# One kernel, its first stage written out by hand: a hybrid encoder layer on one core

## The chip, the cores and the metric

The kernel runs on one core of a Trainium2 chip. A core has TensorE (matrix multiplication, accumulating in PSUM banks of 128 x 512 float32), VectorE, ScalarE and GpSimd, and queues that move data; here SyncE issues all of the transfers. Each engine runs its own list of instructions in order and waits on semaphores for the others. The metric is the device time of one execution in microseconds, lower is better.

## The reference

One layer over 2048 tokens of 1024 channels, all in float32. Only the head of it matters here:

```python
c_act = silu(c)                                   # 1024 values
shift, scale, gate = split(c_act @ ada_w + ada_b, 3)
h = layernorm(x) * (1 + scale) + shift            # 2048 x 1024
q_h, i_h, zf_fw, zf_bw, g_h, q_n, k_n, v_n, g_n = split(h @ w_in)   # 9216 columns
y = concat([hgrn2(q_h, i_h, zf_fw, zf_bw) * silu(g_h), natten(q_n, k_n, v_n, rpb) * silu(g_n)]) @ w_out
out = layernorm(ALPHA * x + gate * y) * ln_g + ln_b
```

`natten` is a two-dimensional neighbourhood attention with 16 heads of 64 channels (handled in 8 pairs), `hgrn2` a gated linear recurrence in both directions with 8 heads of 128. `rpb` is the attention's bias by relative position.

## The kernel before

**Tiling.** The 2048 tokens are two halves of 1024, and each half is two groups (g = 0, 1) of 512 rows. The 1024 channels are eight blocks k of 128. h is kept transposed, channels on partitions, as a sum of a rounded high part and a low part (`hts[g, k, 0]` and `[g, k, 1]`, both float32r, in rows `h`). Weights are split in the same way (`wh`, `wl`), and a product is three matmuls: high by high, low by high, high by low. `proj_mm` (L255) does that for one 128-column block of weights, one k and one group, 512 columns at a time; `vproj` (L268) does it for the attention's values, 256 columns at a time with h as the stationary operand.

**The first stage** (`startup`) makes h of the first half and, with the same steps, the attention's q, k and gate columns of head pair 0 for both groups. The rows of x come in tiles of 128 x 512 (`x_load`). `x_norm` takes their mean and variance on VectorE (L199, L200), makes the rates of four tiles together (L175 to L204) and scales all eight tiles of a group on ScalarE (L208). `h_piece` turns four tiles over with TensorE (L216, out of `ident`), applies shift and scale on ScalarE (L218), copies the high part (L220) and leaves the rest on VectorE (L223).

Shift and scale come from the modulation. `mod_init` makes silu(c), stores it to memory (`c_d`) and loads it back to all partitions (`cb`). `mods(k)` loads two 128 x 1024 blocks of `ada_w` (L144) and multiplies and sums each along its rows on VectorE (L145, rows `ada`). The loop over k does both groups at each k: the sums for k + 1, both groups' pieces for k + 1, then 18 matmuls of 512 columns for k.

**The second stage** (`first_half`) cuts the results into attention operands (`Prep`), runs `vproj` for the first two head pairs, and then goes through the eight pairs: `natten_woven` yields the attention's steps (scores L978 and L981, softmax L990 to L1000, turning L1022, the sums with the values V at L1041), and `weave` puts projections of the next pair between them, in proportion. `slots` holds the small jobs that lie beside: the gate's modulation, the lower bounds of the recurrence (`lower_bounds`), and h of the second half. The values go to memory (`nv`) and come back as `V`, and the bias tables are built in memory (`bias_fill`, `bias_tables`, `bias_pair`).

**What sets the order.** TensorE runs in the order in which the code calls it. The lists of VectorE, ScalarE and SyncE are put together by a scheduler, by its own estimate of when operands are ready; `pinned` operations keep their written order among themselves, and `high_priority` (the weights, `load_split` and `Chunks`) moves an operation up. That is why the first four loads of value weights stand at the head of SyncE's list before. `Chunks` is the feed of weights: four raw buffers (`WR`), split into high and low parts as the buffers of earlier ones come free.

## Time and profile before

| | us |
|---|---|
| median of three timed runs | 2703.81 |
| lowest and highest | 2697.77, 2707.67 |
| the profiled execution | 2706.45 |
| its span, first to last instruction | 2704.6 |
| TensorE busy in it | 2607.9 (96%) |
| VectorE, ScalarE busy | 1763.5 (65%), 1419.8 (52%) |

TensorE is busy for 96% of the span, with a mean granted clock of 0.99, so little is idle, and the place of it counts. The page's slices of 67.6 us show that the first holds most of what is missing. The other engines' shares say nothing by themselves: what they do in the first stage, where TensorE waits for them, is read from their timelines there. Line numbers in the rows below are those of the kernel before; the order of the changed kernel has its own.

### The profile page before, as it was taken

The page shows a single profiled execution, that of the slowest core. Times are in us where ns is not written, and L with a number is a line of the kernel's source. Part 1 is how long each engine was busy: PE and PEld are TensorE (multiplying, and loading weights), DVE is VectorE, ACT ScalarE, POOL GpSimd, SP SyncE. Part 2 cuts the span into 40 slices and gives each one's busy share as a digit, 9 for nine tenths or more (in the row PEclk, how much of TensorE's full clock was granted, in tenths as well). Part 3 has the DMA queues.
Part 4 walks back from the last instruction along what each step waited for, and adds up shares of the span by engine and source line. Part 5 has one row for each costly group of instructions (what it writes and reads, how often), then busy time and mean ns, then how long its engine had stood idle before and what let it go on. Part 6 is the DMA issues. An engine that isn't in the chain of part 4 may idle for free.

```text
span 2704.6 us, 46039 instructions
## 1 busy us (share of the span) xinstructions
PE 2607.9 (96%) x17328; PEld 2154.8 (80%) x17328; DVE 1763.5 (65%) x4351; ACT 1419.8 (52%) x2808; POOL 105.6 (4%) x142
## 2 busy tenths in 40 slices
PE   4999999989999999999999999999999999899998
PEld 3788888878888888888888888887777777678887
DVE  5435445467777778877777877555777778548443
ACT  4434444366666666666666666445666666431110
POOL 0000000000000000000000000000000000032221
PEclk9999999999999999999999999999999999899999
DMA  7565354312111126212221122354444445344331
GB/s 248 158 186 143 128 173 139 116 52 75 63 59 60 64 75 219 79 43 75 75 77 62 65 70 87 102 164 129 123 127 129 126 126 138 109 137 140 98 94 55
DMA packets 226846, 296.46 MB, mean 110 GB/s; under 512 B 28743, under 2 KB 117575, under 8 KB 226503
## 3 DMA queue, kind: packets, MB, share of 16 engines
q1 hardware_dynamic: 226623, 293.52, 35.0%
q8 instruction: 136, 2.23, 0.3%
q14 instruction: 87, 0.71, 0.1%
HBM read 218.24 MB, written 66.99 MB: 105 GB/s over the span
## 4 chain that ended last, share of the span: by engine, by line
PE 71%; DVE 2%; DMA 2%; ACT 1%; SPq 1%; issue 0%; DVEq 0%; ACTq 0%
PE pj L255 39%; PE ps L1333 4%; PE ps L1334 4%; PE ps L1335 4%; PE ps L1041 3%; PE ps L1022 3%; PE ps L455 2%; PE pj L268 2%; PE ps L447 1%; PE ps L978 1%; PE ps L981 1%; PE ps L522 1%; PE ps L546 1%; PE ps L494 1%; PE ps L548 1%; PE ps L620 1%
## 5 line engine op out<-in xcount | busy, mean ns | idle before, releaser
L255 PE MATMUL pj<-h,wh 128*128 128x512 f32 x4016 | 1287.3, 402 | 6.0 <-ACT wh L781 2.1
L255 PEld LDWEIGHTS pj<-h,wh 128*128 128x128 f32 x4016 | 727.4, 189 | 166.6 <-issue 21.5
L255 PE MATMUL pj<-h,wl 128*128 128x512 f32 x2008 | 788.5, 393 | 0.0
L255 PEld LDWEIGHTS pj<-h,wl 128*128 128x128 f32 x2008 | 377.9, 188 | 83.1 <-DVE wl L756 0.4
L995 ACT ACTIVATE pbuf<-pbuf,mx 128x480 f32<-128x480 f32 (+2 forms) x256 | 164.3, 643 | 180.1 <-DVE mx L990 179.4
L990 DVE CUSTOM_DVE_ANT_1 pbuf<-ps,bias 128x480 f32<-128x480 f32 (+2 forms) x256 | 144.0, 595 | 134.4 <-PE ps L981 119.6
L268 PE MATMUL pj<-wh,h 128*128 128x256 f32 x1024 | 197.4, 290 | 4.4 <-ACT vt L274 4.2
L268 PEld LDWEIGHTS pj<-wh,h 128*128 128x128 f32 x1024 | 165.0, 195 | 8.6 <-ACT vt L274 5.1
L245 ACT ACTIVATE wh<-wr 128x512 fp32r<-128x512 f32 x192 | 120.1, 626 | 79.7 <-PE pj L255 69.5
L246 DVE TENSOR_TENSOR wl<-wr,wh 128x512 fp32r<-128x512 f32 x192 | 131.6, 685 | 42.8 <-ACT wh L245 41.8
L268 PE MATMUL pj<-wl,h 128*128 128x256 f32 x512 | 146.5, 286 | 0.0
L1022 PE MATMUL ps<-ident,pbuf 128*128 128x128 f32 x896 | 119.4, 274 | 12.5 <-DVE pbuf L1000 12.5
L1028 ACT ACTIVATE pt<-ps 128x512 f32<-128x512 f32 (+1 forms) x128 | 68.9, 539 | 115.1 <-PE ps L1022 114.9
L1022 PEld LDWEIGHTS ps<-ident,pbuf 128*128 128x128 f32 x896 | 105.4, 141 | 28.6 <-issue 13.6
L1026 DVE COPY pt<-ps 128x512 f32<-128x512 f32 (+1 forms) x128 | 79.3, 620 | 70.1 <-PE ps L1022 69.2
L441 DVE TENSOR_TENSOR de<-e,de 128x512 f32<-128x512 f32 x64 | 44.3, 692 | 118.3 <-ACT de L440 118.3
L1041 PE MATMUL ps<-pt,V 128*64 128x128 f32 x1376 | 105.3, 283 | 7.5 <-DMA V<-nv 3.4
L1000 DVE TENSOR_SCALAR pbuf<-pbuf,mx 128x480 f32<-128x480 f32 (+2 forms) x256 | 107.8, 437 | 5.0
L1041 PEld LDWEIGHTS ps<-pt,V 128*64 128x64 f32 x1376 | 73.8, 137 | 34.8 <-issue 18.6
L1309 ACT ACTIVATE yh<-yr 128x512 fp32r<-128x512 f32 x52 | 32.6, 629 | 130.9 <-PE ps L1334 112.1
L268 PEld LDWEIGHTS pj<-wl,h 128*128 128x128 f32 x512 | 99.8, 195 | 0.7 <-issue 0.5
L1382 DVE TENSOR_TENSOR vt<-ps,gt 128x512 f32<-128x512 f32 x24 | 16.5, 691 | 126.4 <-PE ps L1335 126.4
(268 smaller groups left out, 4623.2 us busy)
## 6 DMA issues: line engine op xcount, KB each, us to landing
wr<-in_w_in SPq DMA_DIRECT2D x276, 256.0 KB
yr<-yq SPq DMA_DIRECT2D x64, 256.0 KB
V<-nv SPq DMA_DIRECT2D x248, 64.0 KB
bias<-tint SPq DMA_DIRECT2D x24, 480.0 KB
wr<-in_w_v SPq DMA_DIRECT2D x32, 256.0 KB
x<-in_x SPq DMA_DIRECT2D x32, 256.0 KB
ada<-in_ada_w SPq DMA_DIRECT2D x16, 512.0 KB
nv<-vt SPq DMA_DIRECT2D x32, 256.0 KB
```

The costliest lines, as they stand in the source:

```text
L245: act.activation(hi, raw, AF.Copy)
L246: dve.tensor_tensor(lo, raw, hi, op=ALU.subtract)
L255: pe.matmul(pz, a, b, start=(k == 0 and n == 0), stop=(k == KT - 1 and n == 2))
L268: pe.matmul(pzs[tp][:, i * 256:(i + 1) * 256], a, b, start=(k == 0 and n == 0 and i == 0), stop=(k == KT - 1 and n == 2), skip_group_check ...
L990: return dve.tensor_tensor_reduce(s[:, 0:nk].rearrange("p (r c) -> p r c", c=32), sc[:, 0:nk].rearrange("p (r c) -> p r c", c=32), bt[:, 0 ...
L995: act.activation(s[:, 0:nk], s[:, 0:nk], AF.Exp, scale=-1.0, bias=mx[:, 0:1], accum_out=mx[:, 1:2])
L1000: dve.tensor_scalar(s[:, 0:nk], s[:, 0:nk], mx[:, 2:3], 1.0, op0=ALU.mult, op1=ALU.mult)
L1022: pe.transpose(ptp[:, c * P:(c + 1) * P], s[:, c * P:(c + 1) * P], ident)
L1041: pe.matmul(self.po[R][hs_, j * P:(j + 1) * P], self.st.V[c0 + c][:, j * P + hh * 64:j * P + hh * 64 + 64], pts[hh][:, c * P:(c + 1) * P], ...
L1333: pe.matmul(pz, yh[:, kk], wh, start=first, stop=False)
L1334: pe.matmul(pz, yh[:, kk], wl, start=False, stop=False)
L1335: pe.matmul(pz, yl[:, kk], wh, start=False, stop=last)
```

## The change

The first stage is written out by hand, and inside it SyncE, ScalarE and VectorE also keep the written order (the lower of the two `manual_schedule` lines). It goes through sixteen steps (g, k), all of group 0 ahead of group 1. A step has a list of small jobs (`jobs`), the transposes and h of the next step, nine matmuls of 512 columns (the gate's weights first), and one k of the first values, twelve matmuls of 256 columns; `vproj` hands back control at each k for that. For k = 0, 1 and 2 the modulation is multiplied by TensorE instead of summed by VectorE: `mod_mm` runs sixteen matmuls of one column, with `ada_p`, laid out for that, as the stationary operand. For the other five `mod_sum` works as before, on one tile of 128 x 2048. The rows of silu(c) lie in the buffer that the bias table uses later.

The second stage loses `vproj`, runs ten projection steps ahead of the first scores (`AHEAD`), takes its small jobs one slot later, and scales the second half's rows in two parts. The small loads of `lower_bounds` and the norm's gain move into the first stage.


The core of the diff:

```diff
+AHEAD = 10
+MPE = 3
...
+    def mod_rows():
+        dma(c_d.rearrange("(p k) -> p k", k=KT), mod["c8"])
+        mod["c"] = tl("nb", shape=[P, 3072])[:, 0:D]
+        dma(mod["c"], c_d.rearrange("(o n) -> o n", o=1).to_broadcast([P, D]))
+
+    def mod_load(k):
+        mod["w", k] = tl("ada", shape=[P, 2 * D])
+        dma(mod["w", k], t["ada_p"][k] if k < MPE else t["ada_m"][k - MPE])
+
+    def mod_mm(k):
+
+        if "p" not in mod:
+            mod["p"] = ps("po")
+        for s in range(2):
+            o = mod["p"][:, 2 * k + s:2 * k + s + 1]
+            for i in range(KT):
+                pe.matmul(o, mod["w", k][:, s * D + i * P:s * D + (i + 1) * P], mod["c8"][:, i:i + 1], start=(i == 0), stop=(i == KT - 1))
+        for s, (dst, bias) in enumerate(((shift, adab), (scale1, adab1))):
+            dve.tensor_tensor(dst[:, k:k + 1], mod["p"][:, 2 * k + s:2 * k + s + 1], bias[:, k:k + 1], op=ALU.add)
+
+    def mod_sum(k):
+        for s, (dst, bias) in enumerate(((shift, adab), (scale1, adab1))):
+            w, c = mod["w", k][:, s * D:(s + 1) * D], slice(k, k + 1)
+            dve.tensor_tensor_reduce(w, w, mod["c"], scale=1.0, scalar=bias[:, c], op0=ALU.mult, op1=ALU.add, accum_out=dst[:, c])
...
+    def vproj(src, dst, half, feed=None, fine=False):
         his, los = feed.take(4) if feed else load_split(lambda i: src[:, i * 512:(i + 1) * 512], 4)
         for t2 in range(2):
...
+                if fine or k % 2:
                     yield None
...
+    lg = cp.tile([P, 16], F32, name="lbl")
+
     def lower_bounds():
-        lg = cp.tile([P, 16], F32, name="lbl")
-        pinned(dma(lg, t["lb_logits"]))
-        dve.tensor_tensor(lbt, lg, lg, op=ALU.subtract)
+        pinned(dve.tensor_tensor(lbt, lg, lg, op=ALU.subtract))
...
-            self.load(WR)
...
-        def split(self):
+        def split(self, ahead=WR):
...
-            self.load(n + 1 + WR)
+            self.load(n + 1 + ahead)
...
-    SB_ = {"cb": 1, "ada": 5, "x": 16, "vo": 2, "nb": 1}
+    SB_ = {"ada": 4, "x": 16, "nb": 1}
...
-    SMS = {"raw": "e", "s": "sg", "w1": "q", "w2": "vt", "w2l": "gt"}
+    SMS = {"raw": "e", "s": "sg", "w0": "bk", "w1": "q", "w2": "vt", "w2l": "gt", "vo": "vt"}
...
+        def w_split(i, a):
+            hi, lo = tl(f"w{i}", F32R), tl("w2l" if i == 2 else f"w{i}", F32R)
+            act.activation(hi, wraw[i][a], AF.Copy)
+            dve.tensor_tensor(lo, wraw[i][a], hi, op=ALU.subtract)
...
+        mod_silu()
+        xs, mvs, how, pts, tmps = {0: x_load(0)}, {0: x_mv()}, {}, {}, {}
+        mod_load(0)
+        w_load(0)
+        feed.load(1)
+        for k in range(1, MPE):
+            mod_load(k)
+        mod_rows()
+        feed.load(2)
+        mod_load(3)
+        w_load(1)
+        feed.load(3)
+        mod_load(4)
+
+        def turn_(g, k):
+            pts[g, k] = h_turn(xs[g], k)
+
+        def high(g, k):
+            tmps[g, k] = h_high(pts[g, k], k, hts[g, k, 0], True)
...
+
+        jobs = {
+            (0, 0): [(w_split, 1, 0), (w_split, 2, 0), (feed.split, 0)],
+            (0, 2): [(feed.split, 0), (scale, 0, 1, 4), (mod_sum, 3)],
+            (0, 3): [(w_split, 0, 1), (w_split, 1, 1), (w_split, 2, 1), (mod_sum, 4)],
+            (0, 4): [(feed.split, 0), (mod_sum, 5)],
+            (0, 5): [(feed.split, 0), (stat, 1, 0), (stat, 1, 1), (mod_sum, 6)],
+            (0, 6): [(mod_sum, 7)],
+            (0, 7): [(stat, 1, 2), (stat, 1, 3), (rates, 1), (scale, 1, 0, 2)],
+            (1, 2): [(scale, 1, 1, 4)],
+        }
+        mod_load(5)
+        feed.load(4)
+        mod_load(6)
+        xs[1], mvs[1] = x_load(1, (0, 1)), x_mv()
+        mod_load(7)
+        xs[1] += x_load(1, (2, 3))
+        acc = {(0, 0): ps("sc"), (1, 0): ps("sc"), (2, 0): ps("po")}
+        values = vproj(t["w_v"][0], nv_d[0], 0, feed, True)
+        rows = {n: [None, None] for n, _ in NCOL0}
+        order = [(g, k) for g in range(2) for k in range(KT)]
+        turn_(0, 0)
+        high(0, 0)
+        w_split(0, 0)
+        low(0, 0)
+        for n, (g, k) in enumerate(order):
+            for f, *a in jobs.get((g, k), []):
+                f(*a)
+            nxt = order[n + 1] if n + 1 < len(order) else None
+            if nxt:
+                turn_(*nxt)
+            late = g == 0 and k + 1 < MPE
+            if nxt and not late:
+                high(*nxt)
+                low(*nxt)
+            if (g, k) == (0, 7):
+                feed.load(8)
+                rp = bias_rows()
                 bias_fill()
+                dma(lg, t["lb_logits"])
+                dma(normg, t["hg_norm_g"])
+            if (g, k) == (1, 0):
+                acc.update({(2, 1): ps("po"), (0, 1): ps("sc"), (1, 1): ps("sc")})
                 bias_tables(rp)
+                bias_pair(0)
+            for i in (2, 0, 1):
+                proj_mm(acc[i, g], *ws[i], g, k)
+            if late:
+                mod_mm(k + 1)
+                high(*nxt)
+                low(*nxt)
+            if k == KT - 1:
+                for i in range(3):
+                    rows[NCOL0[i][0]][g] = evac(acc[i, g])
+            next(values, None)
+            if g:
+                feed.tick()
+        return rows, feed
...
-        for n, _ in NCOL0:
-            for g in range(2):
-                st.piece(n, g)
-        for _ in range(2):
-            feed.free(0)
-        feed.tick()
+        for n, g in (("k", 0), ("k", 1), ("q", 0), ("g", 0), ("q", 1), ("g", 1)):
+            st.piece(n, g)
         for j in (0, 1):
             st.table("top", j)
-        for _ in vproj(t["w_v"][0], nv_d[0], 0, feed):
-            feed.tick()
...
+        slots[0].append((bias_pair, 1))
         for m in range(8):
-            slots[1 + m].append((gate_load, m))
-            slots[3 + m].append((gate_sum, m))
+            slots[2 + m].append((gate_load, m))
+            slots[4 + m].append((gate_sum, m))
         slots[5].append((lower_bounds,))
-        for g, i in ((0, 10), (1, 21)):
+        for g, i in ((0, 11), (1, 22)):
             slots[i].append((rows, g))
-            slots[i + 2].append((norm, g))
+            slots[i + 1].append((stats, g))
+            slots[i + 2 - g].append((scale, g, 0))
+            slots[i + 3 - g].append((scale, g, 1))
             for k in range(KT):
-                slots[i + 3 + k].append((piece, g, k))
+                slots[i + 3 - g + k].append((piece, g, k))
...
-            r = weave(natten_woven(st, nxt, pipe, extra, w == 7), dense, total, steps)[1]
+            r = weave(natten_woven(st, nxt, pipe, extra, w == 7), dense, total, steps, ahead=0 if w else AHEAD * KUS)[1]
...
+        upto(ahead)
         while True:
             try:
                 cum += next(mix)
             except StopIteration as e:
                 tail = e.value
                 break
-            upto(total * share * cum / steps)
+            upto(ahead + (total * share - ahead) * cum / steps)
...
-        with phase("st", SB_, SMS):
+        with phase("st", SB_, SMS), tc.manual_schedule(engines={getattr(mybir.EngineType, e) for e in ("PE", "SP", "Activation", "DVE")}):
...
-    a["ada_w"] = f["ada_w"].reshape(D, 24, P).transpose(1, 2, 0)
+    w = f["ada_w"].reshape(P, KT, 24, P)
+    a["ada_p"] = np.stack([np.concatenate([w[:, :, j].reshape(P, D) for j in (k, KT + k)], 1) for k in range(MPE)])
+    w = f["ada_w"].reshape(D, 24, P).transpose(1, 2, 0)
+    a["ada_m"] = np.stack([np.concatenate([w[k], w[KT + k]], 1) for k in range(MPE, KT)])
+    a["ada_g"] = w[16:]
```

The change moves instructions on three engines. First VectorE's list at the head, where group 0's rows are normalised. Before, behind the last statistics (`bnst`, `xmv`) come the rates (`xr`, `xb`), and then the first sums (`ISA`):

```order
L199 BN_STATS bnst_174<-x_158 128x6
L200 BN_AGGR xmv_161<-bnst_174 128x2
L175 TENSOR_SCALAR v_179<-xmv_161 128x4
L179 TENSOR_TENSOR l_181<-xr_178 128x4
L180 TENSOR_TENSOR l_181<-l_181,v_179 128x4
L181 TENSOR_SCALAR l_181<-l_181 128x4
L182 TENSOR_TENSOR xr_178<-xr_178,l_181 128x4
L204 SCALAR_TENSOR_TENSOR xb_188<-xmv_161,xr_178 128x4
L145 ISA ada_198,shift<-ada_198,cb_144,adab 128x1024
L145 ISA shift 128x1
L145 ISA ada_201,scale_86<-ada_201,cb_144,adab_84 128x1024
```

Now:

```order
L212 BN_STATS bnst_204<-x_163 128x6
L213 BN_AGGR xmv_166<-bnst_204 128x2
L159 TENSOR_TENSOR shift<-ps_208,adab 128x1
L159 TENSOR_TENSOR scale_85<-ps_208,adab_83 128x1
L190 TENSOR_SCALAR v_228<-xmv_166 128x4
L194 TENSOR_TENSOR l_230<-xr_227 128x4
L195 TENSOR_TENSOR l_230<-l_230,v_228 128x4
L196 TENSOR_SCALAR l_230<-l_230 128x4
L197 TENSOR_TENSOR xr_227<-xr_227,l_230 128x4
L219 SCALAR_TENSOR_TENSOR xb_237<-xmv_166,xr_227 128x4
```

The two additions that read TensorE's block from PSUM (`ps_208`) stand ahead of the rates, and the sums of k = 0 are gone from here.

Second, VectorE's list in the k loop. Before, one turn is the low parts of both groups (`h_96` of group 0, `h_112` of group 1) and the two sums for the next k:

```order
L223 TENSOR_TENSOR h_96<-sg_328,h_95 128x512
L223 TENSOR_TENSOR h_112<-sg_337,h_111 128x512
L145 ISA ada_359,shift<-ada_359,cb_144,adab 128x1024
L145 ISA shift 128x1
L145 ISA ada_362,scale_86<-ada_362,cb_144,adab_84 128x1024
L145 ISA scale_86 128x1
L223 TENSOR_TENSOR h_98<-sg_370,h_97 128x512
```

Now, in group 0 between k = 3 (`h_99`) and k = 4 (`h_101`):

```order
L1183 TENSOR_TENSOR h_99<-sg_409,h_98 128x512
L1158 TENSOR_TENSOR bk_435<-e_136,bk_434 128x512
L1158 TENSOR_TENSOR q_439<-e_138,q_438 128x512
L1158 TENSOR_TENSOR gt_443<-e_140,vt_442 128x512
L164 ISA ada_190,shift<-ada_190,nb_179,adab 128x1024
L164 ISA shift 128x1
L164 ISA ada_190,scale_85<-ada_190,nb_179,adab_83 128x1024
L164 ISA scale_85 128x1
L1183 TENSOR_TENSOR h_101<-sg_453,h_100 128x512
```

The turn has one low part instead of two, the same two sums, and here the low parts of three weight splits.

Third, TensorE's list. Before, the last matmuls of k = 0, of both groups' accumulators, are followed by eight transposes for k = 2's pieces:

```order
L255 MATMUL ps_298<-h_109,vt_230 128x512
L255 MATMUL ps_298<-h_110,vt_230 128x512
L255 MATMUL ps_298<-h_109,gt_231 128x512
L216 MATMUL ps_365<-ident,x_133 128x128
L216 MATMUL ps_365<-ident,x_149 128x128
L216 MATMUL ps_365<-ident,x_153 128x128
L216 MATMUL ps_365<-ident,x_157 128x128
L216 MATMUL ps_374<-ident,x_240 128x128
L216 MATMUL ps_374<-ident,x_244 128x128
L216 MATMUL ps_374<-ident,x_248 128x128
L216 MATMUL ps_374<-ident,x_252 128x128
L255 MATMUL pj_293<-h_95,wh_206 128x512
```

Now, at the end of step (0, 0), q's matmuls are followed by the block of k = 1 (`c_141` by `ada_174`) and the values:

```order
L288 MATMUL ps_269<-h_92,q_284 128x512
L288 MATMUL ps_269<-h_93,q_284 128x512
L288 MATMUL ps_269<-h_92,q_285 128x512
L157 MATMUL ps_208<-c_141,ada_174 128x1 x16
L301 MATMUL pj_332<-wh_292,h_92 128x256
L301 MATMUL pj_332<-wl_293,h_92 128x256
L301 MATMUL pj_332<-wh_292,h_93 128x256
L301 MATMUL pj_332<-wh_292,h_92 128x256
```

The transposes of the next step but one come behind the values, and they are four.

## Rows read from the trace of the kernel before

**Rows 1.** first line of the page
```profile
span 2704.6 us, 46039 instructions
```

**Rows 2.** TensorE's waits to 110 us: who for whom, total us, times, longest
```profile
PE ps L216 <- ACT x L208: 33.5, 8, 18.5
```

**Rows 3.** TensorE's timeline: start us, length us, line, operands, count, [idle before]
```profile
36.83 1.33 PE L216 MATMUL ps<-ident,x 128*128 128x128 f32 x5 [0.23 <-ACT x L208]
...
41.09 1.20 PE L255 MATMUL pj<-h,wh 128*128 128x512 f32 x2
...
44.59 0.62 PE L255 MATMUL ps<-h,wh 128*128 128x512 f32 x2
...
47.45 0.70 PE L255 MATMUL pj<-h,wh 128*128 128x512 f32 x2
...
51.66 1.03 PE L216 MATMUL ps<-ident,x 128*128 128x128 f32 x8
...
86.28 0.28 PE L268 MATMUL pj<-wh,h 128*128 128x256 f32 x1
...
109.54 0.33 PE L978 MATMUL ps<-KA,q 128*128 128x352 f32 x1
```

**Rows 4.** the queue of DMA issues (SyncE), timeline
```profile
0.74 1.82 SPq L771 DMA_DIRECT2D wr<-in_w_v  x4
...
122.49 0.97 SPq L276 DMA_DIRECT2D nv<-vt  x2
```

**Rows 5.** VectorE's timeline in the first stage
```profile
9.12 1.30 DVE L199 BATCH_NORM_STATS2 bnst<-x 128x6 f32<-128x512 f32 x2
...
14.21 1.35 DVE L199 BATCH_NORM_STATS2 bnst<-x 128x6 f32<-128x512 f32 x2 [1.54 <-DMA x<-in_x]
...
15.84 0.17 DVE L175 TENSOR_SCALAR v<-xmv 128x4 f32<-128x4 f32 x1
...
47.37 1.28 DVE L145 CUSTOM_DVE_ANT_0 ada<-ada,cb,adab 128x1024 f32<-128x1024 f32 x1
...
49.78 0.08 DVE L145 DVE_READ_ACCUMULATOR2_ANT scale<- 128x1 f32 x1
...
51.96 1.29 DVE L223 TENSOR_TENSOR h<-sg,h 128x512 fp32r<-128x512 f32 x2 [2.10 <-ACT h L220]
```

**Rows 6.** weight loads of one call, and the cheapest matmul (busy us, mean ns)
```profile
576.52 0.97 PEld L455 LDWEIGHTS ps<-v,ke 128*128 128x128 f32 x8 [1.23 <-ACT ke L449]
...
L494 PE MATMUL ps<-qx,kx 128*32 128x64 f32 x1024 | 27.6, 226 | 0.0
```

**Rows 7.** ScalarE's timeline in the first stage
```profile
17.50 5.75 ACT L208 ACTIVATE x<-x,xb,xr 128x512 f32<-128x512 f32 x8 [1.02 <-DVE xb L204]
...
25.90 0.61 ACT L245 ACTIVATE vt<-e 128x512 fp32r<-128x512 f32 x1
26.42 0.61 ACT L245 ACTIVATE q<-e 128x512 fp32r<-128x512 f32 x1
...
39.50 0.76 ACT L218 ACTIVATE sg<-ps,shift,scale 128x512 f32<-128x512 f32 x1
40.29 0.63 ACT L220 ACTIVATE h<-sg 128x512 fp32r<-128x512 f32 x1
```

**Rows 8.** TensorE's timeline behind the values
```profile
133.93 0.70 PE L1041 MATMUL ps<-pt,V 128*64 128x128 f32 x4 [3.45 <-DMA V<-nv]
...
141.11 0.82 PE L1022 MATMUL ps<-ident,pbuf 128*128 128x128 f32 x6
...
173.00 0.39 PE L268 MATMUL pj<-wh,h 128*128 128x256 f32 x1 [3.24 <-ACT vt L274]
```

**Rows 9.** busy us (count) per engine, granted clock, DMA share, in two stretches
```profile
133.93:141.11 7.18, 7.18 (x22) 5.46 (x23) 0.69 (x1) 0.63 (x1) 0.00 (x0) 0.61 0.62 182
175.00:178.00 3.00, 3.00 (x18) 2.78 (x17) 0.00 (x0) 0.32 (x1) 0.00 (x0) 0.65 0.19 61
```

**Rows 10.** VectorE's timeline at the lower bounds
```profile
170.50 0.18 DVE L288 TENSOR_TENSOR lbt<-lbl 128x16 f32<-128x16 f32 x1 [10.68 <-DMA lbl<-in_lb_logits]
```

More of the change, by code (lines that the diff above doesn't have):

```diff
@@ L182, in rstd_of, with x_load @@
         dve.tensor_mul(dst, dst, l)
-    def x_load(g, pre=None):
+    def x_load(g, rows=range(4)):
         xs = []
-        for i in range(4):
-            xt = [pre if pre and i == 0 else tl("x"), tl("x")]
+        for i in rows:
+            xt = [tl("x"), tl("x")]
             r0 = g * GRP + i * P
@@ L192, in x_load, with x_stat, x_rates @@
         return xs
-    def x_norm(xs, on_act=2, pin=lambda x: x):
-        mv = cp.tile([P, 4, 2], F32, tag="xmv", name=nm("xmv"), bufs=2)
-        for i, xt in enumerate(xs):
-            st = cp.tile([P, 2, 6], F32, tag="bnst", name=nm("bnst"), bufs=4)
-            for a in range(2):
-                pin(dve.bn_stats(st[:, a, :], xt[a]))
-            dve.bn_aggr(mv[:, i, :], st)
+    def x_stat(mv, xs, i, pin=lambda x: x):
+        st = cp.tile([P, 2, 6], F32, tag="bnst", name=nm("bnst"), bufs=4)
+        for a in range(2):
+            pin(dve.bn_stats(st[:, a, :], xs[i][a]))
+        dve.bn_aggr(mv[:, i, :], st)
+    def x_rates(mv):
         r = cp.tile([P, 4], F32, tag="xr", name=nm("xr"), bufs=2)
@@ L204, in x_norm, with x_mv, x_stats, x_scale @@
         dve.scalar_tensor_tensor(b, mv[:, :, 0], -1.0, r, op0=ALU.mult, op1=ALU.mult)
-        for a in range(2):
-            for i in range(4):
-                if i < on_act:
-                    act.activation(xs[i][a], xs[i][a], AF.Identity, scale=r[:, i:i + 1], bias=b[:, i:i + 1])
-                else:
-                    dve.tensor_scalar(xs[i][a], xs[i][a], mv[:, i, 0:1], r[:, i:i + 1], op0=ALU.subtract, op1=ALU.mult)
-        return xs
-    def h_piece(xs, k, hi, lo, early=False):
+        return mv, r, b
+    def x_mv():
+        return cp.tile([P, 4, 2], F32, tag="xmv", name=nm("xmv"), bufs=2)
+    def x_stats(xs, pin=lambda x: x):
+        mv = x_mv()
+        for i in range(4):
+            x_stat(mv, xs, i, pin)
+        return x_rates(mv)
+    def x_scale(xs, how, a, on_act=2):
+        mv, r, b = how
+        for i in range(4):
+            if i < on_act:
+                act.activation(xs[i][a], xs[i][a], AF.Identity, scale=r[:, i:i + 1], bias=b[:, i:i + 1])
+            else:
+                dve.tensor_scalar(xs[i][a], xs[i][a], mv[:, i, 0:1], r[:, i:i + 1], op0=ALU.subtract, op1=ALU.mult)
+    def h_turn(xs, k):
         pt = ps("pt")
@@ L1125, in pieces, with w_load @@
-        def pieces(k):
-            for g in range(2):
-                h_piece(xs[g], k, hts[g, k, 0], hts[g, k, 1], True)
-        pieces(0)
-        for k in range(KT):
-            if k + 1 < KT:
-                mods(k + 1)
-                pieces(k + 1)
-            if k == 4:
+        dma(adab, t["ada_b"])
+        ws = [([], []) for _ in NCOL0]
+        wraw = [[tl("raw"), tl("raw")] for _ in NCOL0]
+        feed = Chunks(first_srcs())
+        def w_load(a):
+            for i in range(3):
+                dma(wraw[i][a], t["w_in"][NCOL0[i][1] // P][:, a * 512:(a + 1) * 512])
@@ new lines, in startup, with low, stat, rates @@
+        mod_rows()
[8 more added lines that the diff above has]
+            tmps[g, k] = h_high(pts[g, k], k, hts[g, k, 0], True)
+        def low(g, k):
+            dve.tensor_tensor(hts[g, k, 1], tmps[g, k], hts[g, k, 0], op=ALU.subtract)
+        def stat(g, i):
+            x_stat(mvs[g], xs[g], i)
+        def rates(g):
+            how[g] = x_rates(mvs[g])
@@ new lines, in scale @@
+        def scale(g, a, n):
+            x_scale(xs[g], how[g], a, n)
+        for i in range(4):
+            stat(0, i)
+        mod_mm(0)
+        rates(0)
+        scale(0, 0, 2)
+        jobs = {
[8 more added lines that the diff above has]
+        }
@@ L1146, in startup @@
-        for (i, g), pz in acc.items():
-            raws[NCOL[i][0]][g] = evac(pz)
-        bias_pair(0)
-        bias_pair(1)
-        return raws, feed
+                bias_pair(0)
[6 more added lines that the diff above has]
+            if k == KT - 1:
+                for i in range(3):
+                    rows[NCOL0[i][0]][g] = evac(acc[i, g])
@@ L1170, in rows, with stats, scale @@
             xs[g] = x_load(2 + g)
[L1172 to L1173 removed]
+        how = {}
+        def stats(g):
+            how[g] = x_stats(xs[g], pinned)
+        def scale(g, a):
+            x_scale(xs[g], how[g], a)
         def piece(g, k):
@@ L1216, in drain, with weave @@
                 return e.value
-    def weave(mix, dense, total, steps, last=0):
+    def weave(mix, dense, total, steps, last=0, ahead=0.0):
         got, done, cum = [], [0.0], 0.0
```

60 lines of the change are left out of this document (16 added, 44 removed).

## The prediction

> **What bounds the kernel now.** I read the page's span first, then the waits of TensorE, then its timeline, and only then the other engines. The span is 2704.6 us [rows 1], the profiled run took 2706.45 us (1.85 us lie around the span), and the median of the three timed runs is 2703.81 us, 2.6 us below the profiled one. About 0.5%, 13.5 us, is what can be told from no change here. Nearly everything the change can win is TensorE's idle time at the head: 33.5 us of waits for ScalarE's normalised rows [rows 2]. The dense projections begin at 41.09 us, the eight k steps of both row groups end at 86.28, the first values run from there, and the first attention scores start at 109.54 [rows 3]. That last moment is my milestone, because the same instructions lie behind it in both programs: the orders differ only in the first stage and in the first attention windows. So the sum is: when is the same work done after the change, and which stalls behind the milestone go?
>
> **The price of TensorE's pieces.** Between two sets of transposes eighteen 512-column matmuls take 51.66 - 47.45 = 4.21 us, 0.234 each. The 192 value matmuls take 109.54 - 86.28 = 23.26 us, 0.121 each. Eight transposes cost about 1.0, so four cost 0.5 [rows 3]. A new step (nine matmuls of one group, twelve of the values, four transposes) is 2.1 + 1.45 + 0.5 = 4.05 us; sixteen are 64 us, about what both parts take now. The interleaving itself is worth nothing: it moves work between places where TensorE is busy anyway. The time is decided by when the first step starts and whether the other engines keep up.
>
> **When the first step starts.** The modulation block of k = 0 now waits behind 2 MB of rows, 1 MB of its own. Before, the last of the group's rows came behind the same 3 MB (1 MB of value weights were ahead of them [rows 4]) and was there by 14.21 us [rows 5]; since SyncE then also stood for c's gate, I take 13.7 (12.3 to 14.2). The block is 16 matmuls of one column with 128 x 128 float32 weights. No such matmul is in the trace. A call of four float32 matmuls there shows eight weight loads in 0.97 us, with the last one's 0.19 taken off 0.111 each [rows 6]; so 16 matmuls are 32 loads and 3.5 us at the full clock. Early on, before TensorE has come to its later pace, transposes follow each other at (1.33 - 0.47)/4 = 0.215 us [rows 3], twice those 0.111, which gives 6.9 us. The lower bound is the shortest matmul of the trace, 27.6/1024 = 0.027 us (32 weight columns) [rows 6], which gives 0.9. For the first block, which starts cold, I take 5.2, between the two rows with 128 columns; for the other two 3.5. VectorE now has the two additions of the block ahead of the variance arithmetic, so that waits for TensorE. From 13.7: block 5.2, additions 0.5, variance arithmetic 17.50 - 15.84 = 1.7 [rows 5, 7], two rows scaled by ScalarE at 5.75/8 = 0.72, so 1.4; transposes 0.5; ScalarE's two passes for h, 39.50 to 40.92, 1.4; three weight splits at 0.52, 1.6, because the gate's weights are split last and multiplied first [rows 7]. That makes 26.1 us, against 41.09: 15 us earlier.
>
> **Steps 0 and 1** carry the blocks of k = 1 and 2 on TensorE. Step 0: nine cold matmuls 44.59 - 41.09 = 3.5 [rows 3], block 3.5, additions and h 1.9; the values and the next transposes (1.95) just cover these 1.9. Step 1: 2.1 + 3.5 + 1.9. h of k = 2 is ready at 26.1 + 8.9 + 7.5 = 42.5.
>
> **Steps 2 to 6 are VectorE's.** The lower half of h(k) stands on VectorE ahead of step k's jobs and of the sums for k + 1, and ScalarE can't make h(k + 1) without these sums. One turn of this ring is: lower half 0.65 [rows 5], the jobs, two sums (49.78 + 0.08 - 47.37 = 2.5) [rows 5], h 1.5 [rows 7]. The jobs are 0.7 for one split of value weights (k = 2, 4, 5), 1.9 for three splits (k = 3), and 2.7 for the statistics of two rows of group 1 (k = 5; 1.30 for two halves and a little for gathering them [rows 5]). So the turns are 5.4, 6.6, 5.4, 8.0 and 4.7, in all 30.1 us, where TensorE has 5 x 4.05 = 20.3 to do: it idles 10 us in gaps of 0.7 to 4. Now the same ring serves both groups (47.37 to the next lower halves' end at 51.96 + 1.29), at 5.8 us a step. Group 0 alone hardly makes it shorter, since the sums, its largest part, are paid once per k either way. h of k = 7 is ready at 72.6.
>
> **Step 7.** TensorE's transposes of (1, 0) are written ahead of the nine matmuls of (0, 7), and they wait for two more rows' statistics, the variance arithmetic and the scaling: 0.65 + 2.7 + 1.9 + 1.4 + 0.5, say 7.3 us with the hand-overs. All matmuls of step 7 are queued behind them. Then 3.55 of work, and 2.3 for the clock: after an idle 3.45 us it was granted 0.61 [rows 8, 9], and the gaps here are as long. Group 0 ends at 72.6 + 7.3 + 5.8 = 85.7.
>
> **Group 1** has no sums: 7 x 4.05 + 3.55 = 31.9, and 1.0 where four scalings stand ahead of h(1, 3) on ScalarE. The evacuations (three of rows, two of values, each about as long as a split) lie beside the next step's matmuls; if that cover failed, they would cost about 1.5 us. The milestone comes at **118.6 us, 9.1 later** than now. Starting 15 us earlier is more than eaten by the ring, which used to run for both groups while it stalled.
>
> **Behind the milestone.** Now the first attention sum waits 3.45 us for V, whose last part comes from values stored only after their matmuls [rows 8]. Then from 133.93 to 141.11 only 4 small and 18 large matmuls are started, 4.5 us at the full clock, so 2.7 more go to the low one ([rows 8], 0.61 granted [rows 9]): 6.1 together. After the change ten projection steps run before the first scores and the sum comes some 23 us behind the end of the values (29 projection steps of 0.7, three scores), where V needs about 15: it is 11.4 us now from the store's issue at 122.49 [rows 4] to the stall's end, and some 4 us for the evacuations and the issues ahead. Second, VectorE stands 10.68 us for the small lower-bound load, which it queued in order [rows 10]; ScalarE's value evacuation and TensorE (3.24 us [rows 8]) stand with it, and 1.4 are lost at 0.65 [rows 9] (18 matmuls in 3 us, where 0.121 each would need 2.2). The load moves into the first stage: 4.6. That returns **10.7 us**. The table's five copies, the later order of gates and rows, and the POOL fill of the shared table buffer cost nothing: VectorE has more than three us between the last sums and the copies.
>
> **Sum.** 9.1 - 10.7 = -1.6: span 2703.0, run 2704.9, median about **2702 us**, no change that can be told.
>
> **Rivals.**
> - *Cheap blocks.* If a block costs 0.9 us, as the lower bound has it, the first is 4.3 shorter and the other two 2.6 each: 9.5 us, and 2692; with the 2.3 of clock not lost it is 2690. For it: one column streams. Against it: all 128-column weight loads of the trace are at 0.11. [...] No run here shows a one-column matmul.
> - *The clock (slower).* Group 0 is bursts of matmuls between waits. If TensorE stays at half clock from the first step to (0, 7), a step is 3.9 + 2.9 + 0.9 = 7.7 us and a block 6.9. The first step then starts at 27.8; steps 0 and 1 are 3.9 + 6.9 + 3.8 = 14.6 each; steps 2 to 6 are 7.7, 7.7, 7.7, 8.0, 7.7; step 7 is 7.3 + 6.8; with group 1 (35) the milestone is at 145, and the time 2728. It decides once a step of TensorE is longer than the ring's turn. For it: 3.45 and 3.24 us of waiting each brought a stretch at 0.61 to 0.65 [rows 8, 9]. Against it: while the ring runs now, TensorE is full-speed at short waits. [...]
> - *The stalls stay.* V, the keys copied to the other half or the tables come late again, and nothing of the 10.7 returns: 2713. For it: SyncE's queue is written in order, and the keys' copies land just before the first scores need them. Against: V's margin of 8 us.
>
> **Chances.** Forecast 0.48 (its own range 2696 to 2709), cheap blocks 0.22, clock 0.15, stalls 0.15. Range 2688 to 2719: from cheap blocks with a little more to a half-way clock. Faster by over 0.5% (below 2690.3) needs the cheap blocks and one thing more, or an earlier first block: 0.22. Slower by over 0.5% (above 2717.3) is most of the clock's share and a late first block: 0.17. The rest, 0.61, is within 0.5%.
>
> **What would show it.** Right: first 512-column matmul near 26 us, 32 weight loads per block, TensorE waiting in steps 3 to 7 for ScalarE's h with VectorE busy throughout, a wait of 3 us or more at the transposes of (1, 0), first dense projections of the next head pair near 119, and no wait on V or on the lower-bound load after that. Wrong: steps of group 0 at 4 us (no ring), or a wait for DMA in group 0.

## The result, and the profile after

The changed kernel took 2711.40 us (median of 7 runs, 2708.46 to 2717.37), the kernel before 2703.69. The ratio is 1.0036, 95% interval [1.0020, 1.0051]: slower, by about 0.4%. Beside later experiments it was 1.0027 [1.0017, 1.0038] (2710.31 us, 9 runs). Forecast were 2702 us and no change. The time lies inside the range of 2688 to 2719, but the kernel moved the wrong way, by more than the runs leave open.

The profiled run took 2716.49 us. Its span, then what TensorE waited for up to 130 us (total, times, longest), which answers to [rows 1, 2]:

```profile
core 0 of [0], span 2714.7 us
PE ps L157 <- DMA ada<-in_ada_p: 13.6, 1, 13.6
PE ps L242 <- ACT x L235: 8.1, 4, 4.9
PE ps L288 <- ACT h L249: 5.3, 3, 3.1
PE ps L288 <- ACT vt L1157: 2.2, 1, 2.2
PE pj L288 <- ACT vt L307: 1.1, 1, 1.1
```

The 33.5 us of waits for normalised rows are down to 8.1, and yet the stage is longer. The time went into work. The timeline of TensorE in the same run (start, us, engine, line, operation, tiles, count, idle time before and its releaser) answers to [rows 3]. L157 is the block, L242 the transposes, the rows with `vt` begin the nine matmuls of a step, and the last row is the milestone:

```profile
13.64 6.96 PE L157 MATMUL ps<-c,ada 128*128 128x1 f32 x32 [13.64 <-DMA ada<-in_ada_p]
...
28.00 1.22 PE L288 MATMUL ps<-h,vt 128*128 128x512 f32 x2 [2.24 <-ACT vt L1157]
...
32.64 6.82 PE L157 MATMUL ps<-c,ada 128*128 128x1 f32 x32
...
42.73 1.20 PE L288 MATMUL ps<-h,vt 128*128 128x512 f32 x2
...
45.76 4.74 PE L157 MATMUL ps<-c,ada 128*128 128x1 f32 x32
...
53.77 1.20 PE L288 MATMUL ps<-h,vt 128*128 128x512 f32 x2
...
88.19 0.47 PE L242 MATMUL ps<-ident,x 128*128 128x128 f32 x1 [4.92 <-ACT x L235]
...
89.44 1.20 PE L288 MATMUL ps<-h,vt 128*128 128x512 f32 x2
...
128.59 0.73 PE L288 MATMUL pj<-h,wh 128*128 128x512 f32 x2 [1.10 <-ACT vt L307]
```

The three blocks took 18.5 us where 12.2 were forecast, and the matmuls beside them ran at half speed: nine in 32.64 - 28.00 = 4.64 us (0.3 of it a wait for a weight split), against 72.27 - 70.12 = 2.15 further on in the same run, where 1.00 was granted. The milestone came at 128.59, not at 118.6.

Behind it the forecast held. From 130 to 500 us TensorE waited once:

```profile
PE pj L288 <- ACT wh L813: 2.1, 1, 2.1
```

The waits for V and for the lower-bound load [rows 8, 10] are gone. The clock by stretches of 10 us (the number behind the five engines' busy times; answers to [rows 9]):

```profile
30.00:40.00 10.00, 10.00 (x42) 9.33 (x41) 0.27 (x3) 0.18 (x1) 0.00 (x0) 1.00 0.38 153
40.00:50.00 10.00, 10.00 (x55) 9.41 (x54) 0.69 (x1) 1.23 (x2) 0.00 (x0) 0.90 0.36 131
50.00:60.00 10.00, 10.00 (x52) 9.26 (x52) 6.33 (x12) 7.74 (x12) 0.00 (x0) 0.76 0.84 304
60.00:70.00 10.00, 8.07 (x43) 6.67 (x42) 6.86 (x13) 3.86 (x6) 0.00 (x0) 0.83 0.56 197
...
80.00:90.00 10.00, 4.85 (x21) 3.98 (x20) 5.88 (x17) 3.50 (x7) 2.84 (x2) 0.67 0.00 1
```

Read this view with care: its clock column starts at 1.00 and only means something from the first record, here 44.6 us. Until then the durations tell: 0.22 us for each of the 32 weight loads in a block and 4.64 us for nine matmuls are the lower level, about twice the 2.15 us for nine matmuls at a granted 1.00 and the 0.113 for a load in a block at the full clock (3.63 us for 32, below). From 30 to 50 us TensorE was busy without a gap, and VectorE and ScalarE nearly idle: they waited for the blocks. VectorE's waits for them, to 60 us (the first one includes the wait for the block's load):

```profile
DVE shift L159 <- PE ps L157: 26.6, 3, 9.5
```

### The profile page after: what moved, and what is told of

Same layout as the page of the kernel before. It is cut to its first block, busy times and chain, and to the rows that moved or that the text cites. A ratio compares the mean times of both kernels' runs of the same rounds, so it can differ in the third digit from the quotient of the medians.

```text
span 2714.7 us, 46221 instructions
## 1 busy us (share of the span) xinstructions
PE 2633.0 (97%) x17424; PEld 2180.2 (80%) x17424; DVE 1760.8 (65%) x4349; ACT 1420.2 (52%) x2804; POOL 105.9 (4%) x142
## 4 chain that ended last, share of the span: by engine, by line
PE 72%; DVE 3%; DMA 2%; ACT 1%; issue 0%; SPq 0%; DVEq 0%; ACTq 0%
PE pj L288 39%; PE ps L1442 4%; PE ps L1444 4%; PE ps L1443 4%; PE ps L1073 3%; PE ps L1054 3%; PE ps L488 2%; PE pj L301 2%; PE ps L480 1%; PE ps L1010 1%; PE ps L1013 1%; PE ps L555 1%; PE ps L579 1%; PE ps L527 1%; PE ps L581 1%; PE ps L653 1%
## 5 line engine op out<-in xcount | busy, mean ns | idle before, releaser
L1054 PEld LDWEIGHTS ps<-ident,pbuf 128*128 128x128 f32 x896 | 105.3, 141 | 27.2 <-issue 12.2
```

The costliest lines, as they stand in the source:

```text
L1054: pe.transpose(ptp[:, c * P:(c + 1) * P], s[:, c * P:(c + 1) * P], ident)
```

## The experiments

Two theories could explain the miss. **A**: the blocks cost what they cost because TensorE is at half clock in them and around them. **B**: the clock is beside the point; either a one-column matmul has a price of its own at any clock (the rival of run 1), or the ring of VectorE's sums made the stage late (rival C of run 2). All runs are compared with runs of the kernel before on the same chip (medians 2704.3, 2703.7 and 2704.9 in the three sets). The milestone is the first dense projection of the next head pair, in the profiled execution; in the kernel before, whose order differs, the first scores stand there, at 109.54. In each case it is the 16928th matmul from the end.

| run | edit | us | ratio to before, 95% | milestone |
|---|---|---|---|---|
| again | changed kernel once more | 2710.31 | 1.0027 [1.0017, 1.0038] | 127.27 |
| 1 | TensorE kept busy before the blocks | 2705.52 | 1.0008 [1.0000, 1.0017] | 123.05 |
| 2 | no blocks, all by sums | 2700.31 | 0.9989 [0.9980, 0.9997] | 109.01 |
| 3 | before, with the part behind the stage | 2699.81 | 0.9988 [0.9979, 0.9996] | 109.19 |
| 4 | blocks with 128 equal columns | 2704.41 | 1.0008 [0.9999, 1.0016] | 122.48 |
| 5 | no blocks, lookahead | 2688.14 | 0.9941 [0.9928, 0.9954] | 98.19 |
| 6 | one block instead of three | 2705.38 | 1.0012 [1.0003, 1.0020] | 114.60 |
| 7 | transposes of (1, 0) later | 2710.00 | 1.0023 [1.0014, 1.0033] | 127.48 |
| 9 | run 5, one Exp tied | **2677.62** | 0.9895 [0.9880, 0.9910] | 97.95 |
| 10 | run 3, one Exp tied | 2691.27 | 0.9944 [0.9932, 0.9957] | 108.26 |
| 12 | changed kernel, one Exp tied | 2705.32 | 1.0005 [0.9996, 1.0014] | 128.65 |

**Run 1, a warm TensorE.** Matmuls that nobody reads fill its waits:

```diff
+        def warm(n):
+            for _ in range(n):
+                pe.matmul(wt, ones, fill, start=True, stop=True)
...
+        warm(40)
         mod_mm(0)
+        warm(10)
         rates(0)
```

(and 14 more in step 0.) Expected:

> The changed kernel with idle TensorE filled: 40 matmuls of 512 columns on a constant tile ahead of the first modulation block, 10 behind it, 14 behind the transposes of step (0, 1), ahead of the first projections. Nothing else changes. Theory A (the blocks cost 18.5 us instead of 12.2 because TensorE is at half clock when they run): the first block takes 3.5 to 4.5 us, the second 3.5 to 5, the first projections start near 25 us instead of 28, h of k = 2 is ready near 41 to 43 instead of 52.3, and the time falls by 8 to 12 us, to about 2701. Rival B (a one-column matmul with 128 float32 weight columns has its own price of 0.2 us, whatever the clock): blocks stay at 6 to 7 us, the time stays within 2 us of 2711.

The timeline of TensorE, and stretches of its clock (busy times as above; the last two lie on either side of the moment when it fell in the third block):

```profile
13.53 5.16 PE L157 MATMUL ps<-c,ada 128*128 128x1 f32 x32 [0.46 <-DMA ada<-in_ada_p]
...
29.59 4.10 PE L157 MATMUL ps<-c,ada 128*128 128x1 f32 x32
...
40.25 4.48 PE L157 MATMUL ps<-c,ada 128*128 128x1 f32 x32
...
48.00 1.20 PE L288 MATMUL ps<-h,vt 128*128 128x512 f32 x2
```

```profile
30.00:40.00 10.00, 10.00 (x53) 9.40 (x54) 0.92 (x3) 1.41 (x2) 0.00 (x0) 0.66 0.76 288
40.00:50.00 10.00, 10.00 (x56) 9.56 (x55) 3.67 (x7) 4.76 (x7) 0.00 (x0) 0.66 0.40 141
39.50:42.80 3.30, 3.30 (x28) 3.12 (x27) 0.00 (x0) 0.00 (x0) 0.00 (x0) 1.00 0.00 0
42.80:44.70 1.90, 1.90 (x11) 1.90 (x10) 0.00 (x0) 0.00 (x0) 0.00 (x0) 0.50 0.03 9
```

The blocks sum to 13.7 us instead of 18.5, step 2 begins 5.8 us earlier, and the time falls by 5 to 6 us: A, but half of what it promised (8 to 12 us). The clock, high before the block, fell during it each time (at 15.5, 32.6 and 42.8 us: 0.78 was granted over 10 to 20 us, 0.66 over 30 to 40, 0.50 from 42.8 to 44.7), though TensorE was busy without a gap from 30 to 50 us. Idle time ahead of a block is thus not the whole cause.

**Run 4, wide blocks.** The same block, with its one moving column repeated 128 times:

```diff
...
-pe.matmul(o, mod["w", k][...], mod["c8"][:, i:i + 1], ...)
+pe.matmul(o, mod["w", k][...], mod["c8"][:, i:i + 1].to_broadcast([P, P]), ...)
...
```

> The changed kernel, each of the blocks' matmuls with the same column of silu(c) repeated 128 times as the moving operand, 128 equal output columns, one of which is read. The weight loads are the same in number. Theory A1 (the clock stays low because one-column matmuls leave TensorE's array nearly unused): the clock comes up within the first blocks, the second and third take 3.5 to 4.5 us, the milestone comes near 121, the time 2703 to 2706. Theory A2 (the clock is low only because TensorE idled before each block): the second and third blocks stay at 6.8 and 4.7 us, the time stays within 2 us of 2711 or above.

The same two views:

```profile
13.46 6.25 PE L157 MATMUL ps<-c,ada 128*128 128x128 f32 x32 [13.46 <-DMA ada<-in_ada_p]
...
31.75 3.96 PE L157 MATMUL ps<-c,ada 128*128 128x128 f32 x32
...
40.25 3.73 PE L157 MATMUL ps<-c,ada 128*128 128x128 f32 x32
...
45.83 0.49 PE L288 MATMUL ps<-h,vt 128*128 128x512 f32 x1
```

```profile
21.98:32.23 10.25, 7.04 (x20) 5.06 (x21) 3.54 (x6) 4.57 (x8) 0.00 (x0) 0.50 0.93 343
32.23:40.00 7.77, 7.54 (x55) 6.73 (x55) 0.92 (x3) 1.41 (x2) 0.00 (x0) 1.00 0.54 194
40.00:50.00 10.00, 9.77 (x72) 8.84 (x71) 3.93 (x8) 5.14 (x8) 0.00 (x0) 1.00 0.54 196
```

More arithmetic and less time: the second and third block take 3.96 and 3.73 us, step 2 begins at 45.83 instead of 53.77, and the granted clock stays up from 32.2 us, through both blocks. A1 has its range for the blocks and the time, and misses its milestone (121) by 1.5 us; A2 is out. What the columns do in TensorE's array, the reason that A1 gives, is in no trace. One reservation: the first record of the full clock, at 18.6 us, lies inside the first wide block (6.25 us instead of 6.96), but the rise at 32.2 comes 0.5 us into the second, behind nine matmuls of 512 columns that stand there in the changed kernel too. That rise is not shown to be the wide block's doing; that the clock then stayed up is what sets this run apart from run 1.

**The changed kernel once more.**

> The changed kernel itself once more, on the same chip as the three others, so that they are compared with it and not only with the kernel before: 2708 to 2717 us, ratio to the kernel before 1.002 to 1.005. If its blocks run at half clock by accident of one execution, its profile would show blocks near 3.5 us and a milestone near 119; if not, blocks of 7, 7 and 5 us and a milestone of 128 to 129 again.

Its profile shows both cases:

```profile
13.33 6.96 PE L157 MATMUL ps<-c,ada 128*128 128x1 f32 x32 [13.33 <-DMA ada<-in_ada_p]
...
32.33 6.82 PE L157 MATMUL ps<-c,ada 128*128 128x1 f32 x32
...
45.21 3.63 PE L157 MATMUL ps<-c,ada 128*128 128x1 f32 x32
```

From 43.8 us on, three matmuls of 512 columns took 0.70 us where they had taken 1.28 (31.05 to 32.33), and the clock was not taken back at 48.0 as in the first profile (0.50 there from 48.1 to 54.9; here 1.00 from 50 to 60), so its third block ran at the full clock, in 3.63 us, and one-column matmuls did not bring the clock down there; the first two were slow again, and the milestone, 127.27, moved by 1.3 us. So a block's price is 3.6 to 4.0 at the full clock, with one column moved (3.63) or 128 (3.73 and 3.96), and 6.8 to 7.0 at the half. That is A; a price of 0.2 us a matmul whatever the clock is out.

**Runs 2 and 6, without blocks and with one.** Run 2 sets `MPE` to 0 (and loads the spread c earlier), run 6 sets it to 1; the sums of the other k join the jobs:

```diff
-MPE = 3
+MPE = 1
...
-            (0, 0): [(w_split, 1, 0), (w_split, 2, 0), (feed.split, 0)],
+            (0, 0): [(w_split, 1, 0), (w_split, 2, 0), (feed.split, 0), (mod_sum, 1)],
+            (0, 1): [(mod_sum, 2)],
```

> The changed kernel without TensorE's blocks: all eight modulations are summed on VectorE, the rows of silu(c) are loaded right behind group 0's rows of x, the variance arithmetic no longer waits for TensorE. Theory A: without blocks the first projections start near 20 us, the ring (lower half, jobs, two sums, h) of 4.7 to 8 us a step runs from k = 0, h of k = 7 is ready near 60 instead of 82, the milestone (first projection of the next head pair) comes near 106 instead of 128.6, the time is 2689 to 2693. Rival C (the ring is what made the stage late; three more sums there cost what the blocks did): milestone at 120 or later, the time 2703 or more.

> The changed kernel with one block on TensorE instead of three: k = 1 and 2 by VectorE's sums. If the blocks' price and the half clock around them are the miss: block 0 still 7 us at half clock and first projections at 28; the first matmul of step 2 at 39 to 41 instead of 53.8, milestone 114 to 116 instead of 128.6, time 2700 to 2706. Rival, the blocks of k = 1 and 2 are hidden beside ScalarE's and VectorE's work, and the late start of the first one is the whole cost: step 2 at 50 or later, time 2709 to 2712.

With one block step 2 begins at 38.09 and the milestone at 114.60, both about as A had it; without any, at 32.45 and 109.01. Rival C (a milestone at 120 or later) and the rival of run 6 (step 2 at 50 or later) are out. A block at half clock costs 6.8 us, VectorE's two sums 2.5: TensorE is the slower engine for this work, even where VectorE limits the ring. The times did not follow: run 2 was forecast at 2689 to 2693 and took 2700.31. That opened the question of what runs 2 and 6 lose behind the milestone.

**Run 3, the part behind the stage alone.** To the kernel before: the lower-bound load moved to the start, and ten projection steps ahead of the first scores.

```diff
+    lg = cp.tile([P, 16], F32, name="lbl")
+    dma(lg, t["lb_logits"])
...
-r = weave(natten_woven(...), dense, total, steps)[1]
+r = weave(natten_woven(...), dense, total, steps, ahead=0 if w else AHEAD * KUS)[1]
```

> The kernel before, with only the part behind the first stage: the lower-bound load is issued at the start, and ten projection steps run ahead of the first scores. First stage as before. Theory: both stalls (3.45 us for V, 3.24 us behind the lower bounds) and the half clock behind them go, 10.7 us together, so 2693. Rival D (what the changed kernel won back behind the milestone came from its first stage, where the first group's values are stored earlier): the wait for V stays or moves, at most 5 us are won, 2699 or more.

Both stalls went (only 2.1 us of waits from 110 to 500 us), but 4.5 us were won instead of 10.7. That is rival D's time without its reason, since no wait for V is left; where the rest went, runs 9 and 10 show.

**Run 7, step 7.** The transposes, h and lower half of (1, 0) written behind the matmuls and values of (0, 7):

```diff
-            if nxt:
+            last = (g, k) == (0, 7)
+            if nxt and not last:
                 turn_(*nxt)
...
             next(values, None)
+            if last:
+                turn_(*nxt)
+                high(*nxt)
+                low(*nxt)
```

> The changed kernel with the transposes, h and lower half of (1, 0) written behind the matmuls and values of (0, 7) instead of ahead of them. If the 7.3 us of step 7 are TensorE's queue standing at the transposes of (1,0) while the nine matmuls and twelve of the values are ready: these run from about 83.5 instead of 89.4 and the milestone comes 3.5 to 5.5 us earlier, 123 to 125; time 2706 to 2708. Rival, the idle time only moves behind these matmuls and the clock falls there: milestone 127 or later, time 2710 to 2712.

The timeline of TensorE:

```profile
82.69 0.63 PE L288 MATMUL ps<-h,vt 128*128 128x512 f32 x2
...
87.10 0.33 PE L242 MATMUL ps<-ident,x 128*128 128x128 f32 x1 [0.76 <-ACT x L235]
...
91.56 0.49 PE L288 MATMUL ps<-h,vt 128*128 128x512 f32 x1 [2.77 <-ACT h L249]
```

The rival won. (0, 7) starts 5 us earlier than in the changed kernel's second profile (82.69 against 87.77), but the rows of group 1 are ready no sooner, and TensorE waits 2.77 us behind its work instead of ahead of it, with a half-clock stretch after that (1.48 us for three matmuls at 93.31, 0.85 at 98.36). The milestone is the same. What holds step 7 is VectorE's statistics and what follows from them, not TensorE's queue.

**Run 5, lookahead.** Run 2, with the sums for k + 2 ahead of the lower half of k + 1, so that ScalarE never waits for them, all statistics of group 1 in steps 6 and 7, run 7's edit, and two loads exchanged (against run 2):

```diff
...
-            (0, 1): [(mod_sum, 2)],
-            (0, 2): [(feed.split, 0), (scale, 0, 1, 4), (mod_sum, 3)],
+            (0, 1): [(mod_sum, 3)],
+            (0, 2): [(feed.split, 0), (scale, 0, 1, 4), (mod_sum, 4)],
...
-            (0, 5): [(feed.split, 0), (stat, 1, 0), (stat, 1, 1), (mod_sum, 6)],
-            (0, 6): [(mod_sum, 7)],
+            (0, 5): [(feed.split, 0), (mod_sum, 7)],
+            (0, 6): [(stat, 1, 0), (stat, 1, 1)],
...
```

> The changed kernel without blocks on TensorE (as in the run without blocks: all modulation by VectorE's sums), and with the ring of steps 2 to 7 cut: VectorE sums k + 2 ahead of the lower half of k + 1, all statistics of group 1 stand in steps 6 and 7, the transposes of (1, 0) stand behind the matmuls and values of (0, 7), and the modulation rows of k = 4 are loaded ahead of the second weight halves. If the ring was the sums' wait for the previous h (1.6 us a step of idle VectorE in the run without blocks) and step 7 was the order on TensorE: first projections still at 21.7, a step 4.1 to 4.4 us, (0,7) at about 53 instead of 69.5, the transposes of (1,0) 2 to 3 us late, milestone 94 to 97 (109.0 without lookahead), time 2685 to 2690. Rival, the DMA queues are the bound (they move about 410 GB/s until 45 us): the sums of k = 4 to 7 wait for their rows, milestone 101 to 105, time 2693 to 2697. Rival, what is won at the head is lost again behind the milestone: milestone 94 to 97 and time 2695 to 2700.

The first matmuls of its steps, 2 to 4 and 7 of group 0 and 0 of group 1 behind the first:

```profile
22.22 1.22 PE L290 MATMUL ps<-h,vt 128*128 128x512 f32 x2 [4.89 <-ACT vt L1159]
...
33.49 0.71 PE L290 MATMUL ps<-h,vt 128*128 128x512 f32 x2
...
37.43 0.71 PE L290 MATMUL ps<-h,vt 128*128 128x512 f32 x2
...
41.37 0.71 PE L290 MATMUL ps<-h,vt 128*128 128x512 f32 x2
...
52.84 0.63 PE L290 MATMUL ps<-h,vt 128*128 128x512 f32 x2
...
61.63 1.52 PE L290 MATMUL ps<-h,vt 128*128 128x512 f32 x2 [2.78 <-ACT h L251]
```

A step now takes 37.43 - 33.49 = 3.94 us, which is TensorE's own work, and (0, 7) starts at 52.84 instead of 69.52. The milestone is 98.19, behind the expected 94 to 97, and the time 2688.14, 16 us under the kernel before. The DMA rival is out: VectorE waits once, 1.7 us, for modulation rows. The run has four edits at once, and no run takes them singly. From step 2 to step 5, ahead of the moved statistics and of run 7's edit, it takes 11.8 us where run 2 takes 17.8; this much belongs to the lookahead with the exchanged loads.

**Runs 9, 10 and 12, the lost part behind.** I set the traces side by side by counting TensorE's matmuls from the end. From the 6000th last to the 5000th last, the same instructions in each kernel, it took 138.7 us before, 138.5 and 136.2 in the two profiles after, but 145.1, 143.6, 144.6 and 144.9 in runs 2, 3, 5 and 6. ScalarE in run 5, at that place, 1.8 ms into the program:

```profile
1774.96 0.58 ACT L309 ACTIVATE vt<-pj 128x512 f32<-128x512 f32 x1
1784.59 0.63 ACT L968 ACTIVATE sg<-bk 128x512 f32<-128x512 f32 x1 [9.05 <-DMA bk<-ng]
1785.13 0.58 ACT L309 ACTIVATE vt<-pj 128x512 f32<-128x512 f32 x1
...
1785.76 0.58 PE L303 MATMUL pj<-wh,h 128*128 128x256 f32 x1 [8.75 <-ACT vt L309]
```

The last row is TensorE's. The scheduler had put the Exp of a gate, whose load was late, between the two evacuations of a values step, and TensorE waited 8.75 us for the second. Runs 2, 3 and 6 have it at the same place. In the kernel before and in the changed one that Exp stands three places further on; before:

```profile
1796.55 1.09 ACT L274 ACTIVATE vt<-pj 128x512 f32<-128x512 f32 x2
...
1807.62 0.63 ACT L934 ACTIVATE sg<-bk 128x512 f32<-128x512 f32 x1 [8.98 <-DMA bk<-ng]
```

No line near it had been edited: in ScalarE's list run 6 differs from the changed kernel only by this. In runs 9, 10 and 12 it is tied behind the last evacuation of values that the code has written by then:

```diff
-            act.activation(sg, raw, AF.Exp, scale=-1.0)
+            with tc.issue_after(mod["vt"]) if R == 1 and self.p == 1 else contextmanager(lambda: (yield))():
+                act.activation(sg, raw, AF.Exp, scale=-1.0)
```

> The run with lookahead, and one instruction of ScalarE tied to a later place: the Exp of the second pair's gate (`sg<-bk`, 1.7 ms into the program), which the scheduler had put between the two evacuations of a values step, where it waited 9 us for its load `bk<-ng`, and TensorE 8.8 us for the second evacuation. In the kernel before and in the changed one that Exp stands behind both. If that wait is what the runs without blocks lose far behind the milestone: milestone 98 as before, no wait of `pj` on `vt` over 2 us around 1.76 ms, and 2678 to 2682 us (8.8 less, and some of the half clock behind it). Rival, TensorE waits for something else at that place (keys, V or the next evacuation) or the clock falls there anyway: 2685 to 2690.

> The kernel before with the early lower-bound load and the ten projection steps ahead of the first scores (the run that won only 4.5 of the 10.7 us forecast), with the same Exp tied behind the values' evacuations. If the forecast's 10.7 behind the milestone was right and 8.5 us were lost again at that Exp: 2690 to 2693 us. Rival, the two stalls were worth only 4.5: 2698 to 2701.

> The changed kernel with the same tie alone (its Exp already stood behind both evacuations; it now stands some twenty rows later). A control: if the tie gives nothing by itself, 2708 to 2714 us as the changed kernel (2710 to 2711). Rival, the later place is a gain of its own, and what the other two runs win is not the wait: 2700 to 2706.

The wait went, 0.9 us being left of it:

```profile
PE pj L303 <- ACT vt L309: 0.9, 1, 0.9
```

Run 9 took 2677.62 us, 10.5 less than run 5, run 10 8.5 less than run 3 (by the ratios to the kernel before 12 each); run 10's time is in the expected range, run 9's 0.4 us below it. But the control, run 12, missed its range (2708 to 2714) and landed in its rival's: 2705.32, 5 to 6 us less than the changed kernel. The Exp 27 places later than there is a gain of its own (that piece takes 132.7 us in runs 10 and 12, 134.2 in run 9): where it stood, ScalarE waited 9 us for the load too, with both evacuations done, and TensorE 1.9 us behind it for `pt`; in run 12 neither wait is left. So of what runs 9 and 10 won some 5 to 8 us are put down to the wait between the evacuations (the pieces above, 144 against 136 to 139), the rest to the later place; no run separates the two. Run 9 beats both kernels: 0.9895 [0.9880, 0.9910].

## Why the prediction was wrong

- **The step that failed is the price of the blocks.** It reads "For the first block, which starts cold, I take 5.2 [...]; for the other two 3.5", and steps 0 and 1 were summed with 3.5 of cold matmuls once and the full clock after that. Measured: the first matmul of step 0 came at 28.00 instead of 26.1 (block 6.96). Step 0 took 14.7 us instead of 8.9 (nine matmuls 4.64, block 6.82, and 3.3 from its end to the next step, since the values and transposes there ran cold too). From step 1 to h of k = 2 it took 9.6 instead of 7.5 (block 4.74). In all h of k = 2 came at 51.66 + 0.63 = 52.29, not at 42.5 (ScalarE's row: `51.66 0.63 ACT L249 ACTIVATE h<-sg 128x512 fp32r<-128x512 f32 x1`). That is 9.8 late, 6.3 of it in the blocks themselves and the rest in the cold work beside them, and -1.6 + 9.8 = 8.2 is near what was measured, 6.6 to 7.7 us. The rate was right (3.63 at the full clock); the clock at which the blocks run was not, and run 4, with the same loads, has the second and third block at 3.96 and 3.73. The 3.5 us for nine cold matmuls was a price at a mixed clock: in the trace before, the last three of those nine run from 43.79 to 44.59, at 0.27 each where the cold ones take 0.43.
- **The rival for the clock** had the cause and the wrong extent. It priced a block at 6.9, as measured, but let the half clock last to (0, 7), 2728 us. In steps 2 to 6 VectorE's ring covers a slow TensorE: between h of k = 2 and of k = 7 lie 29.8 us, 30.1 forecast, in spite of half-clock stretches at 65 and 79 us (0.50 granted from 65.1 to 68.4 and from 78.9 to 82.1). The turns (ScalarE's h at 50.85, 56.12, 62.61, 67.88, 75.94, 80.61: 5.3, 6.5, 5.3, 8.1, 4.7) are the forecast's 5.4, 6.6, 5.4, 8.0 and 4.7.
- **The cheap blocks** are out: 3.63 us at the full clock, 0.113 for each of 32 weight loads, beside 0.111 in [rows 6]. Their 0.9 us was an estimate from the shortest matmul of the trace before (0.027 us with 32 weight columns, [rows 6]); a block of 128-column loads takes four times that.
- **Step 7** came 7.4 us after h of k = 7, 7.3 forecast. The sum was VectorE's and ScalarE's work, with step 7's matmuls queued behind it on TensorE; run 7 shows that this queueing is worth 0 to 1 us.
- **Group 1** took 33 us, as forecast, and then TensorE waited 1.1 us for an evacuation of values, which the forecast took as covered (it priced a failure at 1.5).
- **The 10.7 us behind the milestone** were right. The 16000th matmul from the end lies behind both stalls, at 276.4 us before. The changed kernel, 19.1 us late at the milestone, is 8.1 late there, and in its second profile 6.8 after 17.7: 10.9 came back both times. Run 3, 0.35 ahead at the milestone, is 11.3 ahead there, again 10.9; it then lost 4.9 in the piece with the moved Exp, which is why its time seemed to say 4.5. One term does not follow from what it cites, and that the sum came so near is in part luck: the 18 matmuls behind the second stall give 0.8 us, not 1.4; the low level (0.50) was granted from 173.7 to 177.1 us, which is worth 1.7.
- **The ring was accepted as given.** The forecast named VectorE's sums as the bound and still judged the change only by its own order. Run 5 shows what the order left: its lookahead, with three smaller edits, took 12 us off run 2, 10.8 of them ahead of the milestone.

## What to carry to other kernels

Price a short piece of work by the clock it will run at, which was another here when its own instructions changed (run 4: the second block took 3.96 us instead of 6.82), and not by the rate of the same loads inside a dense stretch. Where an engine's list holds a ring (sum, row, lower half), look first whether the next turn's sum can stand ahead of this turn's last step. When a change moves the time less than its stage, line up the two traces from the end and look for the place where they part; an instruction that nobody touched may have changed its place in another engine's list.
